# Seven block products in the up-projection of a transformer layer's MLP, with the MLP's inner tiles and the residual kept in HBM

## The chip, the cores and the metric

The kernel runs on one core of a Trainium2 chip. The metric is device time of one launch in microseconds (us). The core's engines work in parallel, each through its own queue in a fixed order, and wait for one another by semaphores: TensorE (PE) multiplies, VectorE (DVE) and ScalarE (ACT) do elementwise work, GpSimd (POOL) does a little elementwise work and issues DMAs, SyncE (SP) only issues DMAs. Matmuls write PSUM; everything else on chip lies in SBUF; weights lie in HBM.

## The reference

One pre-norm decoder layer on 512 tokens of width 2048: RMSNorm, one input projection, three token mixers, an output projection with residual, a second RMSNorm, a gated MLP, a last RMSNorm. The change concerns the MLP:

```python
def conv_glu_ffn(h, w_up, conv_w, conv_b, w_down):     # h (512, 2048), w_up (2048, 2 x 5632)
    a = h @ w_up
    a = causal_depthwise_conv(a, conv_w, width 3) + conv_b
    gate, up = a[..., :5632], a[..., 5632:]
    return (silu(gate) * up) @ w_down                  # w_down (5632, 2048)
```

## The kernel before

Activations are kept transposed, features on the 128 partitions and the 512 tokens along the row. Every large product is made in float32 precision out of three matmuls on split operands: an operand is `hi` (rounded to float32r, written by ACT, line 81) plus `lo` (the rest, written by DVE, line 82), and a product is hi·hi + hi·lo + lo·hi (lines 95 to 97). Weights come by SP in halves of 8 k-tiles, 128x1024 elements (512 KB), through `stage()`: a `raw` tile (two buffers), then a `hi` and a `lo` tile (four buffers each). A half feeds 24 matmuls of 512 columns.

The program runs through the mixers, then the output projection (`resid()` adds the residual, squares it, scales it by the norm's gain and splits it into `h2`, 16 pairs of k-tiles), then the MLP in four groups of eleven inner tiles. `up(f)` computes one inner tile f: 96 matmuls for the gate block and the up block, the product with the norm's factor `rs2` (line 783), a convolution of one ACT and two DVE instructions per block (lines 784 to 786), silu, the product of the two and its split into `hid`. After eleven of them the group's down-projection adds into the residual tiles `x2[d]`, d = 0 to 15, which stay in SBUF (line 811). In the last group, four of the eleven inner tiles are held back and multiplied in two halves of 256 tokens at the very end (`last()`, lines 841 to 843: 384 matmuls of 256 columns), with the closing norm and the output.

The code is written in program order; a scheduler then sets the order of each engine's queue by its own model of the times, with weight loads and splits at high priority. An engine's queue is worked off strictly in that order, so an instruction that waits holds up all behind it. A tile's buffer is taken again when its last reader is done.

Of the kernel before, what the change touches and what calls it, by code (L numbers as in the profile page):

```python
# [50 lines left out]
def trunk_kernel(ctx: ExitStack, tc: tile.TileContext, xT, consts, onehot, relb, gw, gb, wk, wv,  # L51
                 wst, wai, wiw, wcv, wo, wu, wd, outT):
# [89 lines left out]
    tp = ph1.enter_context(tc.tile_pool(name="tp", bufs=1))  # L142
# [594 lines left out]
    hp = ph2.enter_context(tc.tile_pool(name="hp", bufs=1))  # L737
# [4 lines left out]
    x2, h2 = [], []  # L742
    sacc = hp.tile([P, T], F32, name="sacc", tag="sacc", bufs=1)

    def resid(d, ps):
# [4 lines left out]
        if d < NH:  # L750
# [12 lines left out]
        x2.append(x)  # L763
# [25 lines left out]
    def up(f):  # L789
        pss = [pj(), pj()]  # L790
        for s in range(2):
            accumulate([pss[s]], [tiles_of(wu[2 * f + s])], h2)
        if f == 0:
            ACT.activation(rs2, spread(rstd_cols([sacc], D)), AF.Copy)
        yg = conv(pss[0], f)
        ACT.activation(yg, yg, AF.Silu)
        yu = conv(pss[1], NF + f)
        DVE.tensor_tensor(yg, yg, yu, op=ALU.mult)
        h, l = slot("hidh"), slot("hidl")
        split(yg, h, l)  # L800
        return h, l

    for gidx in range(FG):
        hid = [up(gidx * FT + i) for i in range(FT)]
        if gidx == FG - 1:
            break
# [132 lines left out]
```

## Time and profile before

| | |
|---|---|
| median of 3 runs | 2304.36 us (2304.2 to 2304.61) |
| span of the profiled execution, first to last instruction | 2303.2 us; the runs lie 1.0 to 1.4 us above it, the time around the span |
| PE busy | 2275.0 us, 99% of the span |
| DVE busy | 1217.3 us, 53% |
| ACT busy | 878.4 us, 38% |
| POOL busy | 87.0 us, 4% |
| DMA | 226.49 MB, mean 98 GB/s |
| mean granted clock of PE | 0.995 |

Busy time is the time in which at least one instruction of the engine was under way. Matmuls are pipelined, so their durations overlap; what one costs is the distance from its start to the next one's. The chain of waits goes back from the last instruction to what released it; the engine that holds most of the chain sets the time.

### The profile page before, as it was taken

Reading aid. Unit: us, or ns where it says so; the run is one execution under the profiler, and the core shown is the slowest. Engines: PE = TensorE matmul, PEld = TensorE weight load, DVE = VectorE, ACT = ScalarE, POOL = GpSimd, SP = SyncE. Lnnn points to the kernel's source line nnn. Section 1 sums busy time; section 2 is a strip of 40 time slices with the busy share of each in tenths; the row PEclk is TensorE's granted clock in tenths of the full one; section 3 lists DMA queues with packets and bytes.
Section 4 is the critical chain, followed back from the end, with each engine's and each line's share of the span. In section 5 each row is a group of like instructions: output and inputs, shape, how many; then the busy total and the mean of one; then the engine's idle time right before and its main releaser. Section 6 shows DMA issues by size and latency. Waiting matters only on the chain.

```text
span 2303.2 us, 27199 instructions
## 1 busy us (share of the span) xinstructions
PE 2275.0 (99%) x10788; PEld 1917.5 (83%) x10788; DVE 1217.3 (53%) x1991; ACT 878.4 (38%) x1272; POOL 87.0 (4%) x150
## 2 busy tenths in 40 slices
PE   8999999999999999999999999999999999999998
PEld 7988889888888888888888888888888888888887
DVE  7689576667675335444334444334544433454446
ACT  6536566755564223333223333222333222333223
POOL 4010000000011110000000000000000000000001
PEclk9999999999999999999999999999999999999999
DMA  5333322222233322232333322333233233323233
GB/s 180 103 96 123 100 78 74 74 71 83 89 118 121 101 93 99 92 100 84 95 105 101 101 94 91 91 99 111 92 100 96 84 95 110 101 94 99 71 113 110
DMA packets 72816, 226.49 MB, mean 98 GB/s; under 512 B 9220, under 2 KB 11674, under 8 KB 72688
## 3 DMA queue, kind: packets, MB, share of 16 engines
q1 hardware_dynamic: 67824, 211.40, 28.9%
q0 software_dynamic: 4720, 13.35, 1.7%
q8 instruction: 84, 1.38, 0.3%
q14 instruction: 44, 0.36, 0.1%
q10 hardware_dynamic: 144, 0.01, 0.0%
HBM read 220.50 MB, written 6.18 MB: 98 GB/s over the span
## 4 chain that ended last, share of the span: by engine, by line
PE 94%; DVE 2%; ACT 2%; DMA 1%; issue 1%; POOL 0%; DVEq 0%; ACTq 0%; POOLq 0%
PE pj L95 24%; PE pj L96 24%; PE pj L97 24%; PE mx L95 3%; PE mx L97 3%; PE mx L96 3%; PE pmv L205 1%; PE pmv L207 1%; PE pmv L206 1%; PE pa L440 1%; ACT hi L81 1%; DMA x<-in_xT_dram 1%; PE psc L284 0%; PE ptr L638 0%; DVE lo L82 0%
## 5 line engine op out<-in xcount | busy, mean ns | idle before, releaser
L81 ACT ACTIVATE hi<-raw 128x1024 fp32r<-128x1024 f32 (+5 forms) x438 | 420.3, 960 | 996.5 <-PE pj L96 764.3
L82 DVE TENSOR_TENSOR lo<-raw,hi 128x1024 fp32r<-128x1024 f32 (+5 forms) x438 | 483.7, 1105 | 461.1 <-ACT hi L81 460.7
L95 PE MATMUL pj<-hh,hi 128*128 128x512 f32 x1408 | 547.8, 389 | 0.0
L97 PE MATMUL pj<-hh,lo 128*128 128x512 f32 x1408 | 547.8, 389 | 0.0
L96 PE MATMUL pj<-hh,hi 128*128 128x512 f32 x1320 | 513.5, 389 | 0.0
L95 PEld LDWEIGHTS pj<-hh,hi 128*128 128x128 f32 x1408 | 264.4, 188 | 54.9
L97 PEld LDWEIGHTS pj<-hh,lo 128*128 128x128 f32 x1408 | 264.4, 188 | 54.7
L96 PEld LDWEIGHTS pj<-hh,hi 128*128 128x128 f32 x1320 | 247.9, 188 | 51.3
L95 PE MATMUL pj<-xh,hi 128*128 128x512 f32 (+1 forms) x608 | 232.2, 382 | 0.9 <-ACT ia L250 0.9
L96 PE MATMUL pj<-xl,hi 128*128 128x512 f32 (+1 forms) x608 | 231.7, 381 | 0.0
L97 PE MATMUL pj<-xh,lo 128*128 128x512 f32 (+1 forms) x608 | 231.0, 380 | 0.0
L783 DVE TENSOR_TENSOR a<-pj,rs 128x512 f32<-128x512 f32 x88 | 60.8, 691 | 291.4 <-PE pj L97 289.4
L95 PEld LDWEIGHTS pj<-xh,hi 128*128 128x128 f32 x608 | 114.2, 188 | 19.2 <-ACT ia L250 1.1
L97 PEld LDWEIGHTS pj<-xh,lo 128*128 128x128 f32 x608 | 114.2, 188 | 18.0
L96 PEld LDWEIGHTS pj<-xl,hi 128*128 128x128 f32 x608 | 114.3, 188 | 17.8
L95 PE MATMUL pj<-hidh,hi 128*128 128x512 f32 x320 | 124.5, 389 | 0.0
L96 PE MATMUL pj<-hidl,hi 128*128 128x512 f32 x320 | 124.5, 389 | 0.0
L97 PE MATMUL pj<-hidh,lo 128*128 128x512 f32 x320 | 124.5, 389 | 0.0
L95 PE MATMUL mx<-hidh,hi 128*128 128x512 f32 x320 | 124.5, 389 | 0.0
L96 PE MATMUL mx<-hidl,hi 128*128 128x512 f32 x320 | 124.5, 389 | 0.0
L97 PE MATMUL mx<-hidh,lo 128*128 128x512 f32 x320 | 124.5, 389 | 0.0
L97 PE MATMUL pj<-mh,lo 128*128 128x512 f32 x256 | 99.9, 390 | 0.0
(339 smaller groups left out, 3014.0 us busy)
## 6 DMA issues: line engine op xcount, KB each, us to landing
raw<-in_wu_dram SPq DMA_DIRECT2D x176, 512.0 KB, 3.6
raw<-in_wst_dram SPq DMA_DIRECT2D x76, 512.0 KB, 3.6
raw<-in_wd_dram SPq DMA_DIRECT2D x48, 384.0 KB, 3.1
raw<-in_wo_dram SPq DMA_DIRECT2D x32, 512.0 KB, 3.6
raw<-in_wd_dram SPq DMA_DIRECT2D x48, 320.0 KB, 2.9
x<-in_xT_dram POOLq DMA_DIRECT2D x32, 256.0 KB, 5.7
raw<-in_wcv_dram SPq DMA_DIRECT2D x8, 512.0 KB, 3.7
raw<-in_wai_dram SPq DMA_DIRECT2D x8, 512.0 KB, 3.8
```

Of the source, the lines that this page charges most:

```text
L81: ACT.activation(hi[:, :cols], raw[:, :cols], AF.Copy)
L82: DVE.tensor_tensor(lo[:, :cols], raw[:, :cols], hi[:, :cols], op=ALU.subtract)
L95: PE.matmul(ps, wh, ah[:, lo:], start=first, stop=False)
L96: PE.matmul(ps, wh, al[:, lo:], start=False, stop=False)
L97: PE.matmul(ps, wl, ah[:, lo:], start=False, stop=last)
L205: PE.matmul(ps[t], ah[:, ts], wh, start=(k == 0), stop=False)
L206: PE.matmul(ps[t], al[:, ts], wh, start=False, stop=False)
L207: PE.matmul(ps[t], ah[:, ts], wl, start=False, stop=(k == KT - 1))
L440: PE.matmul(pa[:, c * 192:(c + 1) * 192], x[:, cc * P:(cc + 1) * P], y[:, cc * 192:(cc + 1) * 192], start=(c == 0), stop=(c == 1), skip_gr ...
L783: DVE.tensor_tensor(a, ps, rs2, op=ALU.mult)
```

## The change

The MLP's up-projection is a product of a 2x2 block matrix of weights (gate and up features; first and second half of the contraction, taken as even and odd k-tiles) with a 2x2 block matrix of activations (even and odd k-tiles; first and second 256 tokens). From the third inner tile on it is made with seven block products in place of eight (Winograd's form of Strassen's method), each of 24 matmuls of 256 columns. The first two inner tiles are still made plainly (`up_plain`).

- Sums of activations are made once, into split tiles (`early_sums`, `late_sum`): eight pairs of k-tiles, on DVE and ACT. `late_sum` overwrites a half of `h2`'s even tiles and so comes after the plain tiles' last reading of them.
- Sums of weights are made for each inner tile (`blocks_of`): two by loading a block and letting a POOL DMA add a second block into it, two more in place on DVE. Seven blocks are split instead of four, and five blocks are loaded by SP and two by the adding DMA.
- `up_seven` runs the products in the order a11, a12, s1, s2, s3, s4, a22 and collects the four output blocks out of three PSUM tiles, with three copies by ACT (`part`). The tile `a` takes five products; one copy of it (`u2`) stands between s2 and s3.
- Each inner tile goes to HBM (`hidd`) and comes back before the down-projection, which now runs in three groups of 15, 14 and 15. The residual goes to HBM too (`x2d`) and comes back after the up-projection.
- For the room, `hi` and `lo` have three buffers in place of four; `raw` has three in place of two. This holds for the whole kernel.

```diff
-            raw = wp.tile([P, WS], F32, tag="raw", bufs=2, name="raw")
+            raw = wp.tile([P, WS], F32, tag="raw", bufs=3, name="raw")
...
-            hi = wp.tile([P, WS], F32R, tag="hi", bufs=4, name="hi")
-            lo = wp.tile([P, WS], F32R, tag="lo", bufs=4, name="lo")
+            hi = wp.tile([P, WS + P], F32R, tag="hi", bufs=3, name="hi")
+            lo = wp.tile([P, WS + P], F32R, tag="lo", bufs=3, name="lo")
...
+    def gated(f, ag, au):
+        yg = conv(ag, f)
+        ACT.activation(yg, yg, AF.Silu)
+        yu = conv(au, NF + f)
+        DVE.tensor_tensor(yg, yg, yu, op=ALU.mult)
+        nc.sync.dma_start(hidd[f], yg)
...
+    def early_sums(p):
+        e, o = xs2[2 * p], xs2[2 * p + 1]
+        b11, b12, b21, b22 = e[:, :H], e[:, H:], o[:, :H], o[:, H:]
+        DVE.tensor_tensor(b11, b12, b11, op=ALU.subtract)
+        tcs[p]["s1"] = in_slot(b11, -1)
+        DVE.tensor_tensor(b12, b22, b12, op=ALU.subtract)
+        DVE.tensor_tensor(b11, b22, b11, op=ALU.subtract)
+        tcs[p]["s2"] = in_slot(b11, -1)
+        DVE.tensor_tensor(b11, b11, b21, op=ALU.subtract)
+        tcs[p]["a22"] = in_slot(b11, 1)
+
+    def late_sum(p):
+        (eh, el), e = h2[2 * p], xs2[2 * p]
+        tcs[p]["s3"] = parts_of(eh[:, H:], el[:, H:], e[:, H:], 1)
+
+    up_plain(0)
+    for p in range(KT // 2):
+        early_sums(p)
+    for f in range(1, PLAIN):
+        up_plain(f)
+    for p in range(KT // 2):
+        late_sum(p)
...
+    def blocks_of(src):
+        with tc.high_priority():
...
+            load("s1", rg, "s1", 3, 0)
+            POOL.dma_start(r["s1"], blk(1), accum_op=ALU.add)
+            load("a11", rg, "ra", 2, 2)
+            load("a12", wp, "raw", 3, 3)
+            load("s3", rg, "s3", 3, 0)
+            POOL.dma_start(r["s3"], blk(2), accum_op=ALU.add)
+            load("a22", wp, "raw", 3, 1)
...
+            hl("a11", r["a11"])
+            hl("a12", r["a12"])
+            s = r["s1"]
+            hl("s1", s)
+            DVE.tensor_tensor(s, s, r["a11"], op=ALU.add)
+            hl("s2", s)
+            DVE.tensor_tensor(s, s, r["a12"], op=ALU.add)
+            hl("s3", r["s3"])
+            hl("s4", s)
+            hl("a22", r["a22"])
...
+    def up_seven(f):
+        w = blocks_of(wu[f])
+        ag, au = ft("a"), ft("a")
+        a, b, c = pj([P, H], "pa"), mx([P, H], "pb"), mx([P, H], "pc")
+        product(a, w, "a11", True)
+        p1 = part(a, "sacc")
+        product(b, w, "a12", True)
+        DVE.tensor_tensor(ag[:, :H], b, p1, op=ALU.add)
+        product(c, w, "s1", True)
+        p5 = part(c, "sq")
+        product(a, w, "s2", False)
+        u2 = part(a, "u2")
+        product(a, w, "s3", False)
+        DVE.scalar_tensor_tensor(au[:, H:], a, -1.0, p5, op0=ALU.mult, op1=ALU.subtract)
+        product(c, w, "s4", False)
+        DVE.tensor_tensor(ag[:, H:], c, u2, op=ALU.add)
+        product(a, w, "a22", False)
+        DVE.scalar_tensor_tensor(au[:, :H], a, -1.0, rs2[:, :H], op0=ALU.mult, op1=ALU.mult)
+        DVE.tensor_tensor(au[:, H:], au[:, H:], rs2[:, H:], op=ALU.mult)
+        DVE.tensor_tensor(ag, ag, rs2, op=ALU.mult)
+        gated(f, ag, au)
...
+    def inner(g, i):
+        f = FIRST[g] + i
+        v = hp.tile([P, T], F32, tag=("sacc", "sq", "rs2")[f % 3], bufs=1, name="hidv")
+        nc.sync.dma_start(v, hidd[f])
...
+        split(v, h, l)
+        return h, l
```

How the queues stand at two places. First, ACT's queue in the middle of the up-projection. Before, one inner tile takes four splits (`hi`), two convolutions, a silu and a split of the result:

```order
L81 ACTIVATE hi<-raw 128x1024 x2
L784 ACTIVATE y<-a,cst 128x512
L796 ACTIVATE y<-y 128x512
L81 ACTIVATE hi<-raw 128x1024 x2
L784 ACTIVATE y<-a,cst 128x512
L106 ACTIVATE hidh<-y 128x512
```

Now, for one inner tile, from the copy of a11's product on (`s_9057` holds s1, then s2 and s4; `s_9064` s3, `a_9067` a22; `a_9298` and `a_9300` are the next inner tile's a11 and a12):

```order
L919 ACTIVATE part<-pa 128x256
L890 ACTIVATE hi<-s_9057 128x1024
L805 ACTIVATE y<-y 128x512
L890 ACTIVATE hi<-s_9064 128x1024
L890 ACTIVATE hi<-s_9057 128x1024
L919 ACTIVATE part<-pc 128x256
L890 ACTIVATE hi<-a_9067 128x1024
L919 ACTIVATE part<-pa 128x256
L890 ACTIVATE hi<-a_9298 128x1024
L890 ACTIVATE hi<-a_9300 128x1024
```

The split of a22 now stands ahead of the copy of `a` that s3 waits for. On PE the scheduler has put eleven of s4's 24 matmuls (into `pc`) between s2 and s3 (into `pa`); the rows where they end and s3 begins:

```order
L914 MATMUL pc<-hh,hi 128x256
L915 MATMUL pc<-hh,lo 128x256
L913 MATMUL pc<-hh,hi 128x256
L914 MATMUL pc<-hh,hi 128x256
L913 MATMUL pa<-hh,hi 128x256
L914 MATMUL pa<-hh,hi 128x256
L915 MATMUL pa<-hh,lo 128x256
```

The order of PE's products is therefore a11, a12, s1, s2, eleven of s4, s3, the rest of s4, a22.

Second, DVE's queue between the second plain inner tile and the first one in seven products. Before, one inner tile follows the other:

```order
L783 TENSOR_TENSOR a<-pj,rs_7416 128x512
L82 TENSOR_TENSOR lo<-raw,hi 128x1024
L785 SCALAR_TENSOR_TENSOR y<-a,cst,y 128x511
L786 SCALAR_TENSOR_TENSOR y<-a,cst,y 128x510
L798 TENSOR_TENSOR y<-y 128x512
L107 TENSOR_TENSOR hidl<-y,hidh 128x512
L82 TENSOR_TENSOR lo<-raw,hi 128x1024
```

Now (`x_7219` and `x_7365` are the even tiles of the last two pairs, `a_7870` the first a11 block; L829, L848, L850 and L827 are one pair's sums and their splits, L820 the plain tile's product with `rs2`; between the last two rows stand the plain tile's five remaining DVE instructions):

```order
L827 TENSOR_TENSOR tc<-x_7219,tc 128x256
L829 SCALAR_TENSOR_TENSOR tc<-x_7365,tc 128x256
L848 TENSOR_TENSOR x_7365<-x_7438,x_7365 128x256
L829 SCALAR_TENSOR_TENSOR tc<-x_7365,tc 128x256
L850 TENSOR_TENSOR x_7365<-x_7365,x_7438 128x256
L820 TENSOR_TENSOR a<-pj,rs_7450 128x512
L827 TENSOR_TENSOR tc<-x_7365,tc 128x256
L820 TENSOR_TENSOR a<-pj,rs_7450 128x512
...
L891 TENSOR_TENSOR lo<-a_7870,hi 128x1024
```

All sums of the eight pairs, and the plain tile's elementwise work, stand ahead of the first a11 split. Further ahead in the same queue, after the sums of the first pair alone, stands the first `late_sum` row (`L827 TENSOR_TENSOR hh<-x_6406,hh 128x256`); the other seven follow among the second and third pair's rows.

## Rows read from the trace of the kernel before

**Rows 1.** The page: busy time of PE, and the chain's shares by engine.
```profile
PE 2275.0 (99%) x10788; PEld 1917.5 (83%) x10788; DVE 1217.3 (53%) x1991; ACT 878.4 (38%) x1272; POOL 87.0 (4%) x150
PE 94%; DVE 2%; ACT 2%; DMA 1%; issue 1%; POOL 0%; DVEq 0%; ACTq 0%; POOLq 0%
```
**Rows 2.** Windows (length, busy us by engine, PEclk, DMA share, GB/s): inner tile; mixers.
```profile
1394.34:1416.10 21.76, 21.76 (x97) 18.02 (x96) 10.50 (x12) 6.93 (x9) 0.00 (x0) 1.00 0.31 98
...
264.00:560.00 296.00, 289.02 (x1598) 251.26 (x1597) 198.05 (x456) 183.90 (x302) 4.76 (x9) 1.00 0.24 76
```
**Rows 3.** Timeline in the up-projection (start us, us, engine, line, operation).
```profile
1405.00 0.39 PE L97 MATMUL pj<-hh,lo 128*128 128x512 f32 x1
...
1405.42 0.69 DVE L783 TENSOR_TENSOR a<-pj,rs 128x512 f32<-128x512 f32 x1 [3.35 <-PE pj L97]
...
1416.10 0.39 PE L95 MATMUL pj<-hh,hi 128*128 128x512 f32 x1
```
**Rows 4.** Timeline in the last stage: first matmuls of two tiles, twelve matmuls apart.
```profile
2267.45 0.28 PE L841 MATMUL mx<-hidh,wl_hi 128*128 128x256 f32 x1
...
2268.89 0.28 PE L841 MATMUL pj<-hidh,wl_hi 128*128 128x256 f32 x1
```
**Rows 5.** Groups by line and form, whole span (count, busy us, mean ns, idle before).
```profile
L82 DVE TENSOR_TENSOR lo<-raw,hi 128x1024 fp32r<-128x1024 f32 x300 | 367.5, 1225 | 289.5 <-ACT hi L81 289.3
L81 ACT ACTIVATE hi<-raw 128x1024 fp32r<-128x1024 f32 x300 | 317.8, 1060 | 663.1 <-PE pj L96 585.1 <-PE pmv L206 29.2 <-PE mx L96 16.1
...
L784 ACT ACTIVATE y<-a,cst 128x512 f32<-128x512 f32 x88 | 70.8, 805 | 3.3 <-DVE a L783 3.3
...
L785 DVE SCALAR_TENSOR_TENSOR y<-a,cst,y 128x511 f32<-128x511 f32 x88 | 65.6, 745 | 2.0 <-ACT y L784 1.7
...
L798 DVE TENSOR_TENSOR y<-y 128x512 f32<-128x512 f32 x44 | 30.5, 693 | 1.6
...
L796 ACT ACTIVATE y<-y 128x512 f32<-128x512 f32 x44 | 27.8, 632 | 88.2 <-DVE y L786 88.2
...
L870 DVE SCALAR_TENSOR_TENSOR og<-x,cst,pspr 128x256 f32<-128x256 f32 x22 | 8.8, 477 | 1.6 <-ACT r3s L860 1.6
...
L82 DVE TENSOR_TENSOR lo<-raw,hi 128x1008 fp32r<-128x1008 f32 x4 | 7.0, 1741 | 0.0
...
L845 DVE TENSOR_TENSOR x<-x,pj 128x256 f32<-128x256 f32 x16 | 6.7, 417 | 2.6 <-PE pj L843 2.5
```
**Rows 6.** The tile pmv: ACT's copies of 256 columns from PSUM (ns, minimum/median/maximum).
```profile
L250 ACT ACTIVATE ia<-pmv,rcol x8: 467/472/476, 297.2 to 385.9; 128x256 f32<-128x256 f32 x8
```
**Rows 7.** Timeline of DVE near the end: two instructions back to back.
```profile
2237.36 1.23 DVE L828 TENSOR_TENSOR wl_lo<-rawl,wl_hi 128x1024 fp32r<-128x1024 f32 x1 [2.54 <-ACT wl_hi L827]
2238.51 0.68 DVE L819 TENSOR_TENSOR x<-x,pj 128x512 f32<-128x512 f32 x1
```
**Rows 8.** DMA: a queue (packets, MB, share); issues (count, KB each, us to landing).
```profile
q1 hardware_dynamic: 67824, 211.40, 28.9%
...
raw<-in_wu_dram SPq DMA_DIRECT2D x176, 512.0 KB, 3.6
...
x<-in_xT_dram POOLq DMA_DIRECT2D x32, 256.0 KB, 5.7
...
rawl<-in_wd_dram SPq DMA_DIRECT2D x16, 256.0 KB, 2.9
```
**Rows 9.** Windows near the start, columns as in rows 2, POOL's busy time before PEclk.
```profile
10.00:15.00 5.00, 5.00 (x27) 5.00 (x27) 4.28 (x6) 2.57 (x5) 3.91 (x7) 0.77 1.03 402
...
20.00:25.00 5.00, 3.46 (x12) 3.46 (x13) 5.00 (x4) 2.70 (x4) 5.00 (x4) 0.50 0.37 107
```
**Rows 10.** Timeline of PE around a long wait near the start.
```profile
21.54 0.65 PE L207 MATMUL pia<-lo,xh 128*128 128x336 f32 x1 [4.35 <-DVE lo L82]
21.99 0.48 PE L205 MATMUL pia<-hi,xh 128*128 128x336 f32 x1
...
26.11 0.32 PE L205 MATMUL pia<-hi,xh 128*128 128x336 f32 x1
```

More of the change, by code (lines that the diff above doesn't have):

```diff
@@ L736, in trunk_kernel @@
     ph2 = ExitStack()
-    hp = ph2.enter_context(tc.tile_pool(name="hp", bufs=1))
+    hp = region(ph2, "hp")
+    H = T // 2
+    x2d = dram.tile([KT, P, T], F32, name="x2d")
+    hidd = dram.tile([NF, P, T], F32, name="hidd")
     def ft(name, dt=F32):
         return act.tile([P, T], dt, tag="a", bufs=32, name=name)
-    x2, h2 = [], []
+    xs2, h2 = [], []
     sacc = hp.tile([P, T], F32, name="sacc", tag="sacc", bufs=1)
@@ L749, in resid @@
         g = cst[:, C_NFFN + d:C_NFFN + d + 1]
+        nc.sync.dma_start(x2d[d], x)
         if d < NH:
@@ L762, in resid @@
             POOL.tensor_tensor(sacc, sacc, sq, op=ALU.add)
-        x2.append(x)
+        ACT.activation(x, x, AF.Copy, scale=g)
+        xs2.append(x)
     for d0 in range(0, KT, 2):
@@ L778, in trunk_kernel, with conv @@
     rs2 = hp.tile([P, T], F32, name="rs2", tag="rs2", bufs=1)
-    def conv(ps, i):
+    ORDER = list(range(0, KT, 2)) + list(range(1, KT, 2))
+    hx = [h2[k] for k in ORDER]
+    def conv(a, i):
         cw = cst[:, C_CW + 3 * i:C_CW + 3 * i + 3]
-        a, y = ft("a"), ft("y")
-        DVE.tensor_tensor(a, ps, rs2, op=ALU.mult)
+        y = ft("y")
         ACT.activation(y, a, AF.Identity, scale=cw[:, 2:3], bias=cst[:, C_CB + i:C_CB + i + 1])
@@ L793, in up @@
         if f == 0:
             ACT.activation(rs2, spread(rstd_cols([sacc], D)), AF.Copy)
[L795 to L800, printed above, removed]
-        return h, l
[L803 to L806, printed above, removed]
+        av = []
+        for ps in pss:
+            a = ft("a")
+            DVE.tensor_tensor(a, ps, rs2, op=ALU.mult)
+            av.append(a)
@@ new lines, in up_plain, with parts_of, in_slot @@
+        gated(f, *av)
+    def parts_of(h, l, src, sgn):
+        ACT.activation(h, src, AF.Copy, scale=float(sgn))
+        if sgn > 0:
+            DVE.tensor_tensor(l, src, h, op=ALU.subtract)
+        else:
+            DVE.scalar_tensor_tensor(l, src, -1.0, h, op0=ALU.mult, op1=ALU.subtract)
+        return h, l
+    def in_slot(src, sgn):
+        v = slot("tc")
+        return parts_of(v[:, :H], v[:, H:], src, sgn)
+    tcs = []
+    for p in range(KT // 2):
+        e, o = xs2[2 * p], xs2[2 * p + 1]
+        (eh, el), (oh, ol) = h2[2 * p], h2[2 * p + 1]
+        tcs.append({"a11": (eh[:, :H], el[:, :H]), "a12": (oh[:, :H], ol[:, :H]), "s4": (oh[:, H:], ol[:, H:])})
@@ new lines, in trunk_kernel, with load, hl @@
+    up_plain(0)
[3 more added lines that the diff above has]
+        up_plain(f)
+    for p in range(KT // 2):
+        late_sum(p)
+    s_res.close()
+    s_rg = ExitStack()
+    rg = region(s_rg, "rg", "right")
+    def blocks_of(src):
+        with tc.high_priority():
+            blk = lambda i: src[:, i * WS:(i + 1) * WS]
+            r = {}
+            def load(key, pool, tag, bufs, i):
+                r[key] = pool.tile([P, WS], F32, tag=tag, bufs=bufs, name=key)
+                nc.sync.dma_start(r[key], blk(i))
+            load("s1", rg, "s1", 3, 0)
[5 more added lines that the diff above has]
+            load("a22", wp, "raw", 3, 1)
+            out = {}
+            def hl(key, src):
+                hi = wp.tile([P, WS + P], F32R, tag="hi", bufs=3, name="hi")[:, SH:SH + WS]
+                lo = wp.tile([P, WS + P], F32R, tag="lo", bufs=3, name="lo")[:, SH:SH + WS]
+                ACT.activation(hi, src, AF.Copy)
+                DVE.tensor_tensor(lo, src, hi, op=ALU.subtract)
+                out[key] = hi, lo
+            hl("a11", r["a11"])
[8 more added lines that the diff above has]
+            hl("a22", r["a22"])
+        return out
@@ new lines, in trunk_kernel, with product, part @@
+    NP = KT // 2
+    def product(ps, w, key, first):
+        hi, lo = w[key]
+        for k in range(NP):
+            wh, wl = hi[:, k * P:(k + 1) * P], lo[:, k * P:(k + 1) * P]
+            th, tl = tcs[k][key]
+            PE.matmul(ps, wh, th, start=first and k == 0, stop=False, skip_group_check=True)
+            PE.matmul(ps, wh, tl, start=False, stop=False, skip_group_check=True)
+            PE.matmul(ps, wl, th, start=False, stop=(k == NP - 1), skip_group_check=True)
+    def part(ps, tag):
+        v = hp.tile([P, H], F32, tag=tag, bufs=1, name="part")
+        ACT.activation(v, ps, AF.Copy)
+        return v
@@ new lines, in trunk_kernel @@
+    for f in range(PLAIN, NF):
+        up_seven(f)
+    s_rg.close()
+    rx = region(ctx, "rx", "right")
+    x2 = []
+    for d in range(KT):
+        x = rx.tile([P, T], F32, tag="x", bufs=KT, name="x2")
+        POOL.dma_start(x, x2d[d])
+        x2.append(x)
+    FIRST = [sum(SIZES[:g]) for g in range(3)]
+    def inner(g, i):
+        f = FIRST[g] + i
+        v = hp.tile([P, T], F32, tag=("sacc", "sq", "rs2")[f % 3], bufs=1, name="hidv")
+        nc.sync.dma_start(v, hidd[f])
+        if g == 1:
+            h, l = [hp.tile([P, T], F32R, tag="h", bufs=2 * NH, name="hid") for e in range(2)]
+        else:
+            h, l = slot("hid"), slot("hid")
+        split(v, h, l)
+        return h, l
@@ L807, in trunk_kernel @@
+    hids = [[inner(0, i) for i in range(SIZES[0])], [], []]
+    for g in range(2):
         for d in range(KT):
-            w = tiles_of(wd[gidx * KT + d], FT)
+            w = tiles_of(wd[g][d], SIZES[g])
             ps = mx() if d % 2 else pj()
-            accumulate([ps], [w], hid)
+            accumulate([ps], [w], hids[g])
             DVE.tensor_tensor(x2[d], x2[d], ps, op=ALU.add)
+            if d < SIZES[g + 1]:
+                hids[g + 1].append(inner(g + 1, d))
+    hid = hids[2]
```

46 lines of the change are left out of this document (29 added, 17 removed).

## The prediction

> **What bounds the kernel now.** I read the page first: PE is busy 99% of the span and holds 94% of the chain [rows 1]. So the time is a sum of matmul pitches, and an edit is worth what it takes off PE's stream less the waits it puts into it. Next, windows over one inner tile of the up-projection: in 21.76 us PE never stops, its clock is full, DVE works 10.50 us and ACT 6.93 us, DMA has a share of 0.31 [rows 2]. A 512-column matmul starts every 21.76 / 96 = 0.227 us, though each lasts 0.39 us; the timeline confirms it, with 49 pitches from 1405.00 to 1416.10 [rows 3]. The last stage shows the shape that the change uses, 128x256 with another weight each time: twelve matmuls take 2268.89 - 2267.45 = 1.44 us, 0.120 us each [rows 4]. DVE starts on a product 0.42 us after the start of its last matmul [rows 3], 0.20 us after the next one could start; I use 0.19 us for 256 columns.
>
> **The gain on PE.** An inner tile in seven products is 7 x 24 x 0.120 = 20.16 us in place of 21.76, so 1.60 us less, and 42 x 1.60 = 67.2 us in all. It is less than an eighth because 256 columns cost more than half of 512 (0.120 against 0.113 us).
> The Trainium skill (TensorE: Matmul & The Clock Gate, Back-to-back issue gap) gives columns / 2.4 GHz + 2.5 ns, which is 109 and 216 ns; by that an inner tile would fall from 20.7 to 18.3 us and the gain be 101 us. The rows are 120 and 227 ns for these very shapes, and they decide.
>
> **The steady period: engines.** DVE per inner tile: seven splits and two sums in place of 1024 columns, 9 x 1.225; four convolution steps, 4 x 0.75; six instructions of 256 or 512 columns, together 2.9; the last product 0.69: 17.6 us busy of 20.16. Back to back an instruction starts some 0.08 us before the one ahead ends (2237.36 + 1.23 against 2238.51 [rows 7]), so 16 us. ACT: 7 x 1.06 + 3 x 0.47 + 2 x 0.80 + 0.63 = 11.1 us [rows 5, 6]. Both fit, but not by much; what decides is the order, since each queue waits in turn.
> I step through one period from the moment (0) when a22 of the tile before ends. There are three hi/lo pairs, so a split starts when the product three before it is done. ACT: split of s1 at 0.22 to 1.28, two convolutions to 2.9, copy of a11's product to 3.5. DVE: L939 0.2, lo of s1 1.3 to 2.5, L799 to 3.1, sum for s2 to 4.3, L800 and L799 to 5.6, lo of s2 to 6.7, L800 to 7.4, sum for s4 to 8.6, lo of s3 to 9.7, last product 10.3, lo of s4 to 11.5. PE wants s2 at 8.64, so there is room; it wants lo of s4 at its third matmul of that block, 11.52 + 0.24 = 11.76: 0.2 us of room, the tightest one on DVE.
> The copy u2 has none. s3 adds into the tile that u2 copies, and cover is eleven matmuls of s4, 1.32 us: s3 could start at 12.84. But ACT's queue has the split of a22 first, and that waits for the buffer that s2 frees, hence also for s2's end: 11.52 + 0.19 + 1.06 (split) + 0.03 + 0.47 (copy) = 13.27 us. PE waits 0.43 us, once per inner tile: 42 x 0.43 = **18 us**. Bounds: 0, if s2's end reaches ACT early enough for the copy to fit; 25 us with 0.6 us each. I take 18, the sum of the rows' own durations. What is late next is s4's lo, which may slip another 0.4 us inside this wait.
>
> **The steady period: DMA.** Per inner tile seven blocks of 0.524 MB and a store of 0.262 MB, 3.93 MB. The queue's 211.40 MB took 28.9% of 2303 us, 318 GB/s while busy [rows 8]; near the start a window shows 402 GB/s at a share of 1.03 [rows 9]. So 9.8 to 12.4 us of 20.16, if an adding DMA costs what a plain one does. No row shows one that adds. From below: 1 x, as cheap as plain. From above: no row limits it; a POOL load of 256 KB took 5.7 us against 2.9 from SP [rows 8], 2 x with its start, and I take 2 x: 2 x 0.524 / 318 = 3.3 us more, 15.7 us of 20.16. Then the queues hide it: blocks are loaded about two inner tiles ahead.
> The Trainium skill says that an add inside the DMA engines costs a second source read, which halves the rate, rather than time for the add itself (Collectives: The Full Stack, The bandwidth ceiling). By that the sum is the same 15.7 us; no run here shows it yet.
>
> **Entry into the seven products.** late_sum overwrites what the second plain tile reads last. E is that tile's end on PE. Its second product reads the even k-tiles first, one per 0.68 us from E - 10.9 on, so the eight late rows can run from E - 10.0 to E - 5.3; and since the first of them stands ahead of seven pairs' sums in DVE's and ACT's queues, these wait too. After E - 5.3 about half of the third pair and five whole pairs are left. A pair is a chain of DVE 0.42, ACT 0.47, DVE 0.4 (pitch of a 0.48), 0.42, ACT 0.47, then two pitches of DVE: with 0.03 per hand-over 3.0 us ([rows 5, 6], L845, L870, L250). So E - 2.7 + 5 x 3.0 = E + 12.3; the plain tile's own elementwise work (4.2 us) to E + 16.5; the first lo, 1.23, to E + 17.8. PE can do four matmuls before: **17.5 us** of waiting. The first blocks' loads are little earlier than that: their buffers take the place of the sums' inputs and come free as these are done. After a wait of 4.35 us PE's granted clock was 0.50 (1.2 GHz), and pitches were 0.28 instead of 0.155 us until 26.11 [rows 9, 10]: about 2 us lost, and I add **2 us**. Bounds: 8 us (sums overlap better and half of the work is done by E) and 25 us (blocks land later).
>
> **Exit to the down-projection.** U is the end of the last product. Three inner tiles have room to come back from HBM at a time; a round is 2.9 (load) + 0.63 + 0.69 = 4.3 us for three. The first is split at about U + 4.6, because ACT's and DVE's queues hold the last tile's convolution and silu first, and 1.4 us follow for each next one. The scheduler runs d = 0 and 1 side by side, 6 x 0.227 = 1.36 us of PE per inner tile, so the stream goes on once begun: 4.6 us, with the slow clock after it **6 us** (2 to 14).
>
> **Before the MLP.** Three hi/lo pairs let a split be two halves (10.9 us) ahead, not three (16.3). In the mixers PE idled 296.0 - 289.0 = 7 us of a window [rows 2]; some more idling: **5 us** (-4 to 15). The x2d stores, the 16 scalings (0.7 us of ACT per 10.9 us product), and the coming back of x2 (POOL, needed one product of 10 us later) cost nothing, covered by PE's stream; uncovered they would cost up to one load, 5.7 us.
>
> **Sum.** -67.2 + 18 + 17.5 + 2 + 6 + 5 = -18.7 us. The span becomes 2284.5; with the 1.2 us that the runs lie above it, **2286 us**.
>
> **Rivals.**
> - The covers hold: ACT frees u2 in time, and the mixers lose nothing. -67.2 + 19.5 + 6 = -41.7, 2263 us; without half of the entry's wait 2253. For it: the scheduler placed the eleven matmuls for just this. Against it: ACT's order, read above. Chance 0.22.
> - DVE is the bound (the other side). Its walk to lo of s4 is 11.5 us with 0.6 us until it costs; after that each us of it is a us of PE. With the 30.5 us of single costs, it turns the gain into a loss when a period waits over (67.2 - 30.5) / 42 = 0.87 us, a DVE walk of 11.76 + 0.87 = 12.6 us, 10% longer than its rows. At 15% longer, 13.2 us, the wait is 1.45 us: 2304.4 - 67.2 + 30.5 + 61 = 2329 us. For it: the same split of 1008 columns took 1741 ns at the start while POOL was at work, 42% more [rows 5, 9]; POOL now issues two DMAs per period. Against it: the issues are short, and in the up-projection the split kept to 1225 ns. Chance 0.13.
> - The adding DMA is the bound. 2.88 + 2 k x 0.524 MB at 318 GB/s passes 21.03 us, where all is lost, at k = 3.6; at k = 4 a period is 22.3 us: 2304.4 + 30.5 + 42 x 0.5 = 2356 us. No row speaks for k over 2. Chance 0.08.
> - The seven products don't give what they say, since PE's pitch at 256 columns is worse than 0.120 beside busier DMA and DVE. At 0.1295 the 1.6 us are gone: 2353 us. The last stage held 0.120 with all engines lighter. Chance 0.05.
> - My forecast, 2268 to 2303: chance 0.52.
>
> **How the numbers follow.** Two runs differ by 0.02%; I call a change under 0.2%, 4.6 us, none. Of the forecast's 0.52 about 0.46 is faster by more, 0.05 within, 0.01 slower; the first rival is all faster; the second splits 0.02 faster, 0.02 within, 0.09 slower; the other two are slower. Faster 0.70, same 0.07, slower 0.23. The range leaves out the two slowest rivals' most and the first one's far end: 2250 to 2332.
>
> **What would show it.** In the profile after: pitches of 0.120 us and 42 periods of about 20.6 us; in each one PE's wait before s3 on ACT's copy of `pa`, 0.4 us; one wait of about 17 us ahead of the first lo of a11, on DVE, with the clock at half behind it; a wait of 4 to 5 us where `hid` begins; DMA share about 0.6 to 0.8. A period well over 20.6, with PE waiting for lo of s4 or for s1's or s3's adding DMA, makes the prediction wrong and says by which rival; an entry wait under 8 us makes that term wrong.

## The result and the profile after

The changed kernel takes **2266.3 us** (median; 2263.9 to 2271.0) against 2304.5 us: ratio 0.9838, 95% interval 0.9824 to 0.9852. That is 38.2 us less, about twice the 18.7 us of the forecast. The sign was right, and so was what carries the gain: a shorter stream of matmuls on PE, with stops put into it. The terms of the sum were mis-sized, the matmul's pitch by most and the single costs the opposite way, so that their errors partly cancel. The time lies just under the 2268 to 2303 us that the forecast gave itself.

The page first: its busy times answer to [rows 1], its queues to [rows 8]. The last line is the software queue of before, for comparison.

```profile
span 2262.1 us, 34601 instructions
...
PE 2192.0 (97%) x13812; PEld 1977.2 (87%) x13812; DVE 1497.1 (66%) x2385; ACT 1056.2 (47%) x1539; POOL 171.6 (8%) x250
...
q1 hardware_dynamic: 84240, 260.69, 35.7%
q0 software_dynamic: 18096, 61.59, 13.2%
...
PE 90%; DVE 4%; ACT 3%; DMA 2%; issue 2%; SPq 0%; DVEq 0%; ACTq 0%; POOLq 0%
```

```profile
q0 software_dynamic: 4720, 13.35, 1.7%
```

PE stays the bound with 90% of the chain; DVE, ACT and DMA hold larger pieces than before. Where they lie is read from marks on PE. The timeline of before (first and last mark) and then of after (start us, us, engine, line, operation): first plain product of the up-projection, end of the plain tiles, first of the seven, second tile in seven, last of the seven, first of the down-projection, and a matmul just before the end.

```profile
848.92 0.39 PE L95 MATMUL pj<-hh,hi 128*128 128x512 f32 x1
...
2293.39 0.47 PE L138 MATMUL pspr<-ident,rv 128*128 128x128 f32 x1 [1.28 <-DVE rv L121]
```

```profile
856.19 0.39 PE L102 MATMUL pj<-hh,hi 128*128 128x512 f32 x1
...
900.91 0.39 PE L104 MATMUL pj<-hh,lo 128*128 128x512 f32 x1
924.54 0.58 PE L913 MATMUL pa<-hh,hi 128*128 128x256 f32 x1 [23.24 <-ACT hi L890]
...
953.73 0.28 PE L913 MATMUL pa<-hh,hi 128*128 128x256 f32 x1
...
1756.15 0.28 PE L915 MATMUL pa<-tc,lo 128*128 128x256 f32 x1
1761.45 0.79 PE L102 MATMUL pj<-hid,hi 128*128 128x512 f32 x1 [5.02 <-ACT hid L113]
...
2251.89 0.32 PE L145 MATMUL pspr<-ident,rv 128*128 128x128 f32 x1 [1.27 <-DVE rv L128]
```

From these the sum is made again, with 21.76 us for a plain tile [rows 2] (901.14 and 1756.27 are one pitch after the last start of a stage). It explains the profiled executions, whose spans differ by 41.1 us; the one of after is the fastest of its four runs.

| term | forecast | measured | how |
|---|---|---|---|
| before the MLP | +5 | +7.3 | 856.19 - 848.92 |
| 42 tiles in seven, with the stops in them | -49.2 | -91.8 | (1756.27 - 953.73) / 41 = 19.574 us; 42 x (19.574 - 21.76) |
| entry | +19.5 | +33.0 | 924.54 - 901.14 = 23.4, and the first tile in seven takes 29.19, 9.6 over the mean |
| exit, as what is left | +6 | +10.0 | -41.5 less the three above |
| sum | -18.7 | -41.5 | (2251.89 - 856.19) - (2293.39 - 848.92) + 7.3 |

The steady period. A window over one period, with the columns of [rows 2]. Then PE's starts at the beginning of two products, 24 matmuls apart, answering to [rows 4], and around s4.

```profile
1305.02:1324.46 19.44, 19.33 (x170) 19.13 (x169) 16.20 (x21) 10.19 (x13) 1.75 (x2) 1.00 0.79 208
```

```profile
1305.02 0.28 PE L913 MATMUL pa<-hh,hi 128*128 128x256 f32 x1
...
1307.74 0.28 PE L913 MATMUL pb<-hh,hi 128*128 128x256 f32 x1
...
1316.01 0.28 PE L914 MATMUL pc<-hh,hi 128*128 128x256 f32 x1
1316.40 0.39 PE L915 MATMUL pc<-hh,lo 128*128 128x256 f32 x1
1316.62 0.29 PE L913 MATMUL pc<-hh,hi 128*128 128x256 f32 x1
...
1317.55 0.28 PE L913 MATMUL pa<-hh,hi 128*128 128x256 f32 x1
```

(1307.74 - 1305.02) / 24 = **0.1133 us** is the pitch of 128x256, where the last stage had 0.120. The stop of the period stands at the first `lo` matmul of s4, 0.39 and 0.22 us in place of two pitches, 0.38 us in all; s3 (1317.55) follows s4's eleventh matmul without one. DVE at this place:

```profile
1314.53 0.69 DVE L807 TENSOR_TENSOR y<-y 128x512 f32<-128x512 f32 x1
1315.13 1.22 DVE L891 TENSOR_TENSOR lo<-s,hi 128x1024 fp32r<-128x1024 f32 x1
```

`lo` of s4 ends at 1316.35, and PE goes on at 1316.40. Not every period is like this: of 40 from one `pb` product to the next, 29 take 19.4 us, seven 19.8 and four 20.1. In the long ones the pitch goes to 0.118 us behind a stop of s4. In the next period `lo` of s4 comes in time, and PE stops ahead of s3 instead, by 0.32 us in the 20.1 us periods (s4's eleventh matmul starts at 1180.35, s3 at 1180.69 and its second matmul at 1180.91); each stretch that ends before the stage does ends at such a stop.

The entry. DVE and ACT at the end of the plain tile, then the chain of waits from there, then the granted clock (column after POOL's time) in the stretches behind the two long waits:

```profile
918.47 0.69 DVE L807 TENSOR_TENSOR y<-y 128x512 f32<-128x512 f32 x1
924.52 1.22 DVE L891 TENSOR_TENSOR lo<-a,hi 128x1024 fp32r<-128x1024 f32 x1 [5.36 <-ACT hi L890]
```

```profile
923.43 2.01 ACT L890 ACTIVATE hi<-a 128x1024 fp32r<-128x1024 f32 x2 [5.79 <-DMA a<-in_wu_dram]
```

```profile
916.65 12.10 DMA s<-in_wu_dram
...
929.29 10.04 DMA s<-in_wu_dram
```

```profile
924.54:928.20 3.66, 3.50 (x14) 3.21 (x15) 2.34 (x2) 0.90 (x1) 0.00 (x0) 0.50 1.06 276
941.76:945.02 3.26, 2.72 (x12) 2.42 (x12) 2.26 (x2) 1.17 (x2) 0.00 (x0) 0.53 1.05 274
```

DVE is done with the sums and the plain tile at 919.16, E + 18.0; the forecast had E + 16.5. But the first block of a11 lands at 923.4, and s3, whose adding DMA is issued when the plain load has landed, at 939.4. The split of s4 stands behind that of s3 in its queues, so PE makes a second stop, of 3.7 us and ahead of s4, that the forecast did not have. Behind each stop the granted clock is at about half (1.2 GHz), as it is behind the exit's wait (0.50 from 1761.45 to 1764.60). The DMA share is over 1 there: the transfers came late and all at once.

### The profile page after: what moved, and what is told of

Its sections match the earlier page's. It is cut to its first block, busy times and chain, and to the rows that moved or that the text cites. A ratio compares the mean times of both kernels' runs of the same rounds, so it can differ in the third digit from the quotient of the medians.

```text
span 2262.1 us, 34601 instructions
## 1 busy us (share of the span) xinstructions
PE 2192.0 (97%) x13812; PEld 1977.2 (87%) x13812; DVE 1497.1 (66%) x2385; ACT 1056.2 (47%) x1539; POOL 171.6 (8%) x250
## 3 DMA queue, kind: packets, MB, share of 16 engines
q0 software_dynamic: 18096, 61.59, 13.2%
## 4 chain that ended last, share of the span: by engine, by line
PE 90%; DVE 4%; ACT 3%; DMA 2%; issue 2%; SPq 0%; DVEq 0%; ACTq 0%; POOLq 0%
PE pj L102 11%; PE pj L103 11%; PE pj L104 11%; PE pa L913 7%; PE pa L915 7%; PE pa L914 7%; PE pc L915 4%; PE mx L103 3%; PE mx L104 3%; PE mx L102 3%; PE pc L913 3%; PE pc L914 3%; PE pb L915 2%; PE pb L913 2%; PE pb L914 2%
## 5 line engine op out<-in xcount | busy, mean ns | idle before, releaser
L88 ACT ACTIVATE hi<-raw 128x1024 fp32r<-128x1024 f32 (+5 forms) x238 | 235.2, 990 | 507.5 <-PE pj L103 297.5
L89 DVE TENSOR_TENSOR lo<-raw,hi 128x1024 fp32r<-128x1024 f32 (+5 forms) x238 | 272.4, 1146 | 237.3 <-ACT hi L88 235.6
L890 ACT ACTIVATE hi<-s 128x1024 fp32r<-128x1024 f32 x168 | 177.8, 1059 | 190.9 <-PE pa L914 68.6
L891 DVE TENSOR_TENSOR lo<-s,hi 128x1024 fp32r<-128x1024 f32 x168 | 204.7, 1219 | 31.0 <-ACT hi L890 31.0
L913 PE MATMUL pa<-hh,hi 128*128 128x256 f32 x672 | 188.6, 281 | 23.7 <-ACT hi L890 23.2
L914 PE MATMUL pa<-hh,hi 128*128 128x256 f32 x672 | 187.6, 279 | 0.0
L915 PE MATMUL pa<-hh,lo 128*128 128x256 f32 x672 | 187.5, 279 | 0.0
L915 PE MATMUL pa<-tc,lo 128*128 128x256 f32 x672 | 186.2, 277 | 0.0
L913 PE MATMUL pa<-tc,hi 128*128 128x256 f32 x672 | 186.2, 277 | 0.0
L914 PE MATMUL pa<-tc,hi 128*128 128x256 f32 x672 | 186.2, 277 | 0.0
L891 DVE TENSOR_TENSOR lo<-a,hi 128x1024 fp32r<-128x1024 f32 x126 | 154.2, 1225 | 30.9 <-ACT hi L890 27.0
L913 PEld LDWEIGHTS pa<-hh,hi 128*128 128x128 f32 x672 | 127.8, 190 | 25.7 <-ACT hi L890 23.7
L914 PEld LDWEIGHTS pa<-hh,hi 128*128 128x128 f32 x672 | 127.8, 190 | 0.0
```

The source lines that it names most:

```text
L890: ACT.activation(hi, src, AF.Copy)
L891: DVE.tensor_tensor(lo, src, hi, op=ALU.subtract)
L913: PE.matmul(ps, wh, th, start=first and k == 0, stop=False, skip_group_check=True)
L914: PE.matmul(ps, wh, tl, start=False, stop=False, skip_group_check=True)
L915: PE.matmul(ps, wl, th, start=False, stop=(k == NP - 1), skip_group_check=True)
```

## The experiments

**Where the weights lie, alone.** The weight tiles of the seven products were put at an offset of 80 columns in their buffers; I had read over that.

```
-SH = 80
+SH = 0
```

> The one edit is SH = 0 in place of 80: the weight tiles of the seven products start at column 0 of their buffers, as those of the plain products do. Theory A (where the weights lie in SBUF sets the pitch: 0.120 us with offset 0 in the last stage, 0.1133 to 0.1178 us with offset 80 in the seven products): the pitch goes to 0.120 us, a period from the 19.60 us measured on average to 168 x 0.120 = 20.16 us or a little more, and the time from 2266 to 2266 + 42 x 0.56 = 2290 us. Theory B (the pitch comes from something else that the seven products have and the last stage has not, such as the order of the weights or the halves of the moving tiles): the pitch stays at 0.113 to 0.118 us and the time within 2262 to 2271 us.

Measured 2297.7 us (2296.9 to 2300.5), ratio 0.9976 (0.9966 to 0.9985). Starts of two products, 24 matmuls apart, then s4's first `lo` matmul, its eleventh and s3; DVE's split of s4; ACT's copy u2:

```profile
1301.56 0.28 PE L913 MATMUL pa<-hh,hi 128*128 128x256 f32 x1
...
1304.44 0.28 PE L913 MATMUL pb<-hh,hi 128*128 128x256 f32 x1
...
1313.32 0.28 PE L915 MATMUL pc<-hh,lo 128*128 128x256 f32 x1
...
1314.28 0.28 PE L914 MATMUL pc<-hh,hi 128*128 128x256 f32 x1
1314.60 0.38 PE L913 MATMUL pa<-hh,hi 128*128 128x256 f32 x1
```

```profile
1311.67 1.21 DVE L891 TENSOR_TENSOR lo<-s,hi 128x1024 fp32r<-128x1024 f32 x1
```

```profile
1314.18 0.37 ACT L919 ACTIVATE part<-pa 128x256 f32<-128x256 f32 x1
```

2.88 / 24 = 0.120 us. Theory A holds. A period is 20.4 us, 0.28 us of it a stop, and here the stop stands where the forecast put it. `lo` of s4 ends at 1312.88, 0.44 us before PE takes it; the copy u2 ends at 1314.55, and s3 starts at 1314.60 in place of 1314.40, its second matmul 0.1 us late too. This is the kernel that I had priced, and it gains 6.5 us, less than my 18.7: its tiles gain 6 us more than forecast, the entry costs 13 us more, and the mixers and the exit the rest.

**The offset for the plain tiles too.**

```
-            hi = wp.tile([P, WS + P], F32R, tag="hi", bufs=3, name="hi")
+            hi = wp.tile([P, WS + P], F32R, tag="hi", bufs=3, name="hi")[:, SH:SH + WS]
(and lo alike, in stage())
```

> The offset of 80 columns is given to the plain weight tiles as well (stage()), nothing else. Theory A (the offset takes 0.0067 us off each matmul, whatever its columns): the pitch of 512 columns falls from 0.2267 to 0.220 us; 4356 matmuls of 512 columns and 384 of 384 columns go through these tiles, so 4740 x 0.0067 = 32 us, and the time becomes about 2235 us, less if the mixers, where PE waits for others too, give only part. Theory B (at 512 columns the weight load is hidden whole, so where it reads from does not matter): pitch 0.2267 us and 2262 to 2271 us.

Measured 2283.3 us (2281.4 to 2284.1), 17 us slower than the changed kernel: neither theory. Starts in the down-projection:

```profile
1999.67 0.39 PE L102 MATMUL pj<-hid,hi 128*128 128x512 f32 x1
...
2000.37 0.40 PE L102 MATMUL pj<-hid,hi 128*128 128x512 f32 x1
```

0.2333 us (the whole stretch has it; 0.70 / 3 here) in place of 0.2267. The offset that speeds 256 columns up slows 512 down. So which offset for which shape?

**Two sweeps.**

```
+OFF = {"a11": 0, "a12": 16, "s1": 32, "s2": 48, "s3": 64, "s4": 96, "a22": 112}
(each product's tiles at OFF[key]; the plain tiles at 0, 16, ... 112 in turn; the second sweep with other numbers; one execution each)
```

> A measurement, not a version: each of the seven products gets an offset of its own for its weight tiles (a11 0, a12 16, s1 32, s2 48, s3 64, s4 96, a22 112 columns), and the plain tiles go through 0, 16, ... 112 in turn, so that the pitch at each offset is read from one trace. The two offsets measured so far: 256 columns 0.120 us at 0 and 0.1133 us at 80; 512 columns 0.2267 us at 0 and 0.2333 us at 80. Theory A1 (the place of the weights within 512 bytes sets the pitch): the products fall into at least two pitches by their offset, a11 at 0.120 us, with the plain tiles changing pitch with the count of the tile. Theory A2 (only 0 and not 0 matter): all but a11 at 0.1133 us and all plain halves but every eighth at 0.2333 us. Theory C (it is the distance between the hi and lo tiles, not the offset): one pitch for all, since both are shifted alike.

Starts of a22 (112), a11 (0), a12 (16), s1 (32) and s2 (48), each 24 matmuls after the one before:

```profile
1297.45 0.28 PE L917 MATMUL pa<-tc,hi 128*128 128x256 f32 x1
1300.28 0.28 PE L917 MATMUL pa<-hh,hi 128*128 128x256 f32 x1
1303.17 0.28 PE L917 MATMUL pb<-hh,hi 128*128 128x256 f32 x1
1305.90 0.28 PE L917 MATMUL pc<-tc,hi 128*128 128x256 f32 x1
1308.73 0.28 PE L917 MATMUL pa<-tc,hi 128*128 128x256 f32 x1
```

0.118, 0.120, 0.114 and 0.118 us; s2 has 0.118 too. In the down-projection, starts of halves at offsets 96, 112, 0 and 16, 24, 21, 24 and 21 matmuls long:

```profile
1834.40 0.39 PE L106 MATMUL pj<-hid,hi 128*128 128x512 f32 x1
...
1839.98 0.40 PE L106 MATMUL pj<-hid,hi 128*128 128x512 f32 x1
...
1844.79 0.40 PE L106 MATMUL mx<-hid,hi 128*128 128x512 f32 x1
...
1850.25 0.40 PE L106 MATMUL mx<-hid,hi 128*128 128x512 f32 x1
...
1855.15 0.39 PE L106 MATMUL pj<-hid,hi 128*128 128x512 f32 x1
```

0.2325, 0.2290, 0.2275, 0.2333 us. Theory A1 holds, in a finer form: what counts is the offset modulo 64 columns, 256 bytes: of the eight offsets of the plain tiles 0 and 64 are alike, 16 and 80, 32 and 96, 48 and 112. The program lays the weight tiles, and the tiles of activations that they are multiplied with, all at 64 bytes past a multiple of 256. Whether the weights' own address counts, or its distance from the activations', was not tried.

> A measurement again: finer offsets, a11 8, a12 24, s1 4, s2 12, s3 20, s4 40, a22 56 columns, and the plain tiles go through 4, 8, 12, 20, 24, 28, 40, 56 in turn. The first sweep gave, in columns modulo 64: 256 columns 0.120 us at 0, 0.1133 at 16, 0.118 at 32 and 48; 512 columns 0.227 at 0, 0.233 at 16, 0.232 at 32, 0.229 at 48. Theory A (a place within 256 bytes sets the pitch, in steps of a few columns): values between these, none below 0.1133 and 0.2267 us by more than 0.002 us. Rival: somewhere between the coarse steps both shapes are faster, down towards the 0.107 and 0.213 us that 256 and 512 columns at 2.4 GHz would take alone.

Between the coarse steps 256 columns took 0.117 to 0.120 us and 512 columns 0.231 to 0.234: nothing below 0.1133 and 0.2267. Of the offsets tried, the changed kernel has the best one for each shape, 16 for 256 columns and 0 for 512.

**The entry: one more plain tile, and a11 first.**

```
-PLAIN = 2
+PLAIN = 3
```

> PLAIN = 3: one more plain inner tile between the early sums and the seven products. Theory (the entry's wait of 23.4 us is the rest of the early sums, about five pairs of 3 us, behind which the blocks' loads wait too): 21.8 us more of PE's work let the sums end in time; what is left of the 33 us of entry (23.4 us wait and 9.6 us in the first seven) is the late sums and the blocks that follow them, 8 to 14 us; the third plain tile costs 21.76 - 19.57 = 2.2 us. 2266 - 33 + 11 + 2 = 2246 us. Rival (the wait is set by the blocks, whose buffers come free only with the late sums behind the last plain tile): a wait of about 20 us stays, and the time is 2262 to 2268 us.

Measured 2254.0 us (2247.7 to 2254.7), 12 us less: the wait ahead of a11 falls from 23.24 to 5.89 us, so most of it was the sums; the stop ahead of s4 stays at 3.47 us. I expected 2246. Of the 8 us that are missing some 4 are the entry, of which 15 us are left in place of 11, and 3.5 are longer periods: 23 of 39 take 19.8 to 20.1 us here.

```
+            load("a11", rg, "ra", 2, 2)
             load("s1", rg, "s1", 3, 0)
             POOL.dma_start(r["s1"], blk(1), accum_op=ALU.add)
-            load("a11", rg, "ra", 2, 2)
```

> a11's block is allocated and loaded before s1's, nothing else. In the after trace DVE was done with the sums 18.0 us after the plain tile's end, but a11's load was issued only 14.2 us after it, behind the loads of three s1, and landed 22 us after it. Theory (the last 4 us of the entry's wait are that load): the wait falls from 23.4 to about 19 us, where DVE's queue ends, and the time by 4 us, to 2262 us. Rival (s1 and s3 are later by the same time and give it back in the first seven products): 2266 us, with the wait short and the stop ahead of s4 longer than 3.95 us.

Measured 2266.3 us (2262.7 to 2272.6), no change. The waits on PE ahead of a11 and s1:

```profile
919.42 0.58 PE L913 MATMUL pa<-hh,hi 128*128 128x256 f32 x1 [18.19 <-ACT hi L890]
...
932.27 0.58 PE L913 MATMUL pc<-tc,hi 128*128 128x256 f32 x1 [4.80 <-ACT hi L890]
```

The first wait shrinks as the theory has it, by 5 us, and s1 gives it back, as the rival has it, though not at s4, where 3.26 us are left. The entry is a stock of transfers that all wait for the buffers of the sums' inputs; their order only moves the wait.

**The stop in the period.**

```
-        DVE.tensor_tensor(yg, yg, yu, op=ALU.mult)
+        POOL.tensor_tensor(yg, yg, yu, op=ALU.mult)
```

> The product of the two branches (512 columns, one per inner tile, 0.69 us of DVE just ahead of lo of s4 in its queue) is moved from DVE to POOL. Theory: lo of s4 is late by 0.27 us in most periods because DVE's walk to it is 11.33 us; with 0.6 us less in front of it the wait in s4 goes, 33 periods x 0.27 = 9 us, 2257 us, and a period is 168 x 0.1133 = 19.04 us and a little. Rival: POOL's operation takes 1.06 to 1.80 us where the trace has it, stands ahead of the issue of an adding DMA and works beside DVE, so s1 or s3 come late or DVE's instructions get longer: no gain or a loss, 2266 us and over.

Measured 2282.0 us (2281.5 to 2283.6), 16 us slower. POOL's product, and DVE's split of s4 beside it:

```profile
1319.76 3.24 POOL L807 TENSOR_TENSOR y<-y 128x512 f32<-128x512 f32 x1 [7.79 <-DVE y L800]
```

```profile
1320.63 1.22 DVE L891 TENSOR_TENSOR lo<-s,hi 128x1024 fp32r<-128x1024 f32 x1
...
1322.10 1.98 DVE L891 TENSOR_TENSOR lo<-s,hi 128x1024 fp32r<-128x1024 f32 x1
```

The split of s3, which lies wholly beside POOL's product, keeps its 1.22 us; that of s4, under way when the product ends, takes 1.98. It is so in all 40 periods; why the one and not the other is not shown. `lo` of s4 is late by 0.8 us. This is the DVE rival of the prediction, brought about by hand, and it costs what such a wait costs.

```
-        DVE.tensor_tensor(yg, yg, yu, op=ALU.mult)          # in gated(f)
+            DVE.tensor_tensor(s[:, :T], yg, yu, op=ALU.mult)    # in up_seven(f + 1), s: its s block, after lo of s4
+            nc.sync.dma_start(hidd[pf], s[:, :T])
```

> The product of the two branches stays on DVE, but is written into the buffer of the next inner tile's s blocks, so that it must follow lo of s4 in DVE's queue; ahead of lo of s4 there stands now the add of pb's product (0.33 us in DVE's stream) in place of it (0.60 us). Theory: lo of s4 is late by 0.27 us in most periods because of DVE's walk, so this takes away just that: a period of 19.44 us goes to 19.17 us, 33 x 0.27 = 9 us, 2257 us. It is also the counterpart of the run with POOL, where DVE's split beside POOL took 1.98 in place of 1.22 us. Rival (s4 waits for something else that ends at the same time, such as the copy of pc's product or its buffers): no change, 2266 us.

Measured 2257.4 us (2257.3 to 2257.6): the number expected, but not its way. PE around s4, and ACT's copy of `pa`, u2:

```profile
1293.91 0.38 PE L917 MATMUL pc<-hh,lo 128*128 128x256 f32 x1
...
1294.94 0.28 PE L916 MATMUL pc<-hh,hi 128*128 128x256 f32 x1
1295.19 0.39 PE L915 MATMUL pa<-hh,hi 128*128 128x256 f32 x1
```

```profile
1293.81 1.06 ACT L892 ACTIVATE hi<-a 128x1024 fp32r<-128x1024 f32 x1 [1.13 <-issue]
1294.78 0.37 ACT L921 ACTIVATE part<-pa 128x256 f32<-128x256 f32 x1
```

`lo` of s4 comes nearly in time now, and the next wait steps forward: s3 stops for u2's copy, which stands behind the split of a22, as the prediction had it. Of the period's 0.39 us of stops 0.13 are left at s4 and 0.26 stand at s3, so the period stays at 19.4 us. What is gained is that all 40 periods take 19.4 us and none 19.8 or 20.1: their mean is 19.43 us, and 41 x (19.57 - 19.43) = 6 us of the 9. The profiled executions differ by no more than that (2263.9 and 2257.6 us); the rest is that the median of the changed kernel lies 2.4 us above its profiled run.

**Parking alone, and half of the tiles.**

```
-PLAIN = 2
+PLAIN = 44        (and no early and late sums)
```

> PLAIN = 44: all inner tiles of the up-projection are plain, and the early and late sums are left out; what stays of the change is the parking of the residual and of the gated tiles in HBM, three hi/lo pairs in place of four, the wider raw ring and the down-projection's three groups. My theory takes the one-off costs outside the seven products as 5 us in the mixers and 6 us at the exit: 2304.5 + 11 = 2315 us. If the after trace's own figures hold (the chain's marks in the mixers stand 2.7 us later, PE waits 6.9 us for hid and starts again at half clock): 2312 to 2316 us. Rival, the parking costs nothing or saves something since PE's stream hides it: 2304 us or less.

Measured 2320.5 us (2319.2 to 2323.1), ratio 1.0073 (1.0058 to 1.0088). The up-projection starts at 855.43, 6.5 us after that of before, and from there to the end mark it is 7.8 us more. So the parking and the third hi/lo pair cost 16 us, where I had 5 + 6.

> PLAIN = 23, so 21 inner tiles in seven products in place of 42, and nothing else: it separates what a tile gives from what is paid once. If a tile gives 21.76 - 19.57 = 2.19 us (measured in the after trace) and the entry, the exit and the mixers are paid once: 2266.3 + 21 x 2.19 - 20 (the early sums are long done at the entry, as with PLAIN = 3, where 12 us were saved beyond the 2.2 us of one more plain tile) = 2292 to 2300 us. If a tile gave what I forecast (1.17 us) and the rest came from elsewhere: 2266.3 + 24.6 - 14 = 2277 us.

(PLAIN = 23, no other edit.) Measured 2291.6 us (2290.7 to 2292.8). From PLAIN = 3 that is 37.6 us for 20 tiles, 1.9 us each: not the forecast's 1.17, and below 2.19, since four of 19 periods are long here and 23 of 39 there.

**Together.**

```
PLAIN = 3; the late product of the branches; wl_hi and wl_lo of last() at the offset of 80 columns
```

> The version that the runs so far point to: the product of the branches behind lo of s4 (2257.4 us alone), PLAIN = 3 (12 us less alone), and the offset of 80 columns for the weights of the last stage too, whose 384 matmuls of 256 columns have 0.120 us at offset 0: 384 x 0.0067 = 2.6 us. If the three add up: 2257.4 - 12.3 - 2.6 = 2242.5 us. Rival: the parts overlap (the first seven products after a third plain tile wait for blocks, not for DVE): 2248 us or more.

Measured **2243.8 us** (2243.0 to 2244.7), ratio 0.9739 (0.9724 to 0.9755): the parts add up, and it beats both kernels. (In the last stage the pitch became 0.118, not 0.1133, so that part gave under 1 us. The program lays `wl_lo` right behind `wl_hi`, 16 x 512 + 80 = 8272 columns on, which is 16 more than a multiple of 64; so the same offset of 80 puts `wl_lo` where 32 is in the sweep. That this is the reason was not tried.)

```
-        u2 = part(a, "u2")
+        u2 = hp.tile([P, H], F32, tag="u2", bufs=1, name="part")
+        DVE.tensor_copy(u2, a)
```

> The joint version (2243.8 us) with one edit more: the copy u2 of a's sum after s2 is made by DVE, behind the late product of the branches, in place of ACT, where it stands behind the split of a22. In the run with the late product the lateness of lo of s4 had shrunk, but PE stopped for 0.25 us ahead of s3, where it had to wait for that copy on ACT (1294.78 to 1295.15 us; PE went on at 1295.19 in place of 1294.93). Theory (this is the wait that I had forecast for u2, hidden so far behind the one for s4): on DVE the copy can end at about 1295.0, the stop ahead of s3 falls to 0.1 us, and 41 periods x 0.15 = 6 us go: 2238 us. Rival (the other order that follows on DVE makes a lo later, or a third wait takes its place): 2243 us or more.

Measured 2249.5 us (2248.5 to 2249.7), slower: the rival. With the copy on DVE the scheduler put s3 after five matmuls of s4 in place of eleven, so the copy's end, early as it was, was too late again by 0.3 us; and 16 of 39 periods are long ones, 19.6 to 20.1 us.

## Why the prediction was half right

- **The gain on PE** is the step that failed: "0.120 us each", taken from the last stage [rows 4] as the row of "the shape that the change uses". It was the same shape at another offset. With offset 80 the pitch is 0.1133 us, with offset 0 it is 0.120 (first experiment). A period without its stops is 168 x 0.1133 = 19.04 us, not 20.16. With the eleven long ones a period takes 19.57 us on average, of which 0.39 are stops; so the pitches take 19.18 us, 0.98 less than forecast, and 42 x 0.98 = 41 us are nearly the whole surplus of the term (91.8 - 49.2 = 42.6).
- By the formula of the Trainium skill (TensorE: Matmul & The Clock Gate, Back-to-back issue gap: columns / 2.4 GHz + 2.5 ns) the gain before waits was 101 us, by estimate. The runs lie nearer to that total, 42 x (21.76 - 19.18) = 108 us, but not because the formula holds: 256 columns took 0.1133 to 0.120 us against its 0.109, and 512 columns 0.2267 to 0.234 against its 0.216. That section of the Trainium skill gives it for a matmul by itself, without the load of its weights; here each matmul has a load of its own (13812 of PE and of PEld on the profile's page).
- **The stop of 0.43 us per period**: right in size (0.38), wrong in place. The forecast called `lo` of s4 the tightest on DVE, wanted at its ninety-ninth pitch; at 0.1133 in place of 0.120 us that moment is 98 x 0.0067 = 0.65 us earlier, and DVE's walk could not follow. The stop that it makes is the time in which u2's copy gets done. The late product shows both: with one gone, the other stands there. So does SH = 0: at the 0.120 us of the forecast `lo` of s4 is in time, and the stop stands ahead of s3 on u2's copy, 0.28 us.
- **DMA**: right. Queue q0 took 13.2% of 2262 us for 61.59 MB, before 1.7% of 2303 us for 13.35 MB; less the time of before, and that of 4.19 MB of x2 at the old rate, the adding DMAs took 247 us for 44.0 MB, 178 GB/s. That is 1.8 to 1.9 times the price of the plain ones (323 GB/s on q1, 341 on q0 before), where the forecast took 2 x, and the queues hid it in the steady stretch. The trace agrees with the half rate that the Trainium skill gives for an add that needs two source reads (Collectives: The Full Stack, The bandwidth ceiling), measured there on a ring's ReduceScatter.
- **Entry**, 19.5 forecast, 33.0 measured, outside its bounds of 8 to 25: the sums' chain with the plain tile's work behind it was right within 1.5 us. I had dismissed the blocks in one sentence ("little earlier than that"); they end the wait 5 us later, and s3's plain load with an adding one behind it makes a second stop with a second stretch at half clock.
- **Mixers and exit**: 7.3 and 10.0 in place of 5 and 6, inside their bounds; the parking alone shows 6.5 and 7.8.
- **The rivals**: "the covers hold" gave the right time (2263) by luck: its cover did not hold, and PE stops in every period. Neither DVE nor the adding DMA became the bound.

Left open: why the place of the weights changes the pitch, and why a stretch of periods runs at 0.118 us in some executions and kernels and not in others. Such stretches begin and end at a stop. The profiled run of the late product has none, and its runs lie together (2257.3 to 2257.6); the one with the offset everywhere has none either, though its seven products are those of the changed kernel, whose runs spread over 7 us.

## What to carry to other kernels

A pitch read from another stage is a price for that stage's addresses too: look at where the operands lie before taking it over, and if a diff moves them, keep that as an unknown. When PE gets faster, every deadline of the helpers moves forward with it, so the walk of each queue has to be made again at the new pitch. A wait behind which buffers come free costs its own length and then the transfers that start only at its end.

## What the runs showed of the hardware that was not expected

- The place of the weight tile modulo 256 bytes changes the pitch of float32r matmuls here: 256 columns 0.120, 0.1133, 0.118, 0.118 us at 0, 16, 32, 48 columns from the tile's start; 512 columns 0.2267, 0.2333, 0.2325, 0.2290. Of these four, the best offset for one shape is the worst for the other. At 16 columns, stretches of the changed kernel run at 0.118 us.
- A POOL multiplication of 128x512 beside a busy DVE took 3.1 us on average, where DVE had taken 0.69 for it. It stretched the DVE split that was under way when it ended from 1.22 to 1.98 us, and left one that lay wholly beside it at 1.22.
